# Two weight sums made by DMA chains, and the third product ahead of the fourth in a group's last pair

## The chip, the cores and the metric

The kernel runs on one core of one Trainium2 chip. The metric is the device time of one execution in microseconds (us). [...] In the rows of the profile, PE is the matrix engine and PEld its weight loads, DVE the vector engine, ACT the scalar engine, POOL the engine that here only issues the adding DMAs, and SP the one that issues the plain loads. Each engine works through its own list of instructions in order. An instruction that waits holds up everything behind it on its engine.

## The reference, cut to what matters

An encoder of two layers over 528 tokens (16 learned ones and 512 given ones) of width 1024. Each layer has two feed-forward blocks and a mixer between them; four feed-forward blocks in all.

```python
def swiglu(x, w_gate, w_up, w_down):
    return (jax.nn.silu(x @ w_gate) * (x @ w_up)) @ w_down

for l in range(DEPTH):                       # DEPTH = 2, D_FF = 2816
    h = h + 0.5 * swiglu(rmsnorm(h, norm_gains[l, 0]),
                         ffn_w_gate[l, 0], ffn_w_up[l, 0], ffn_w_down[l, 0])
    h = h + mixer(rmsnorm(h, norm_gains[l, 1]), ...)
    h = h + 0.5 * swiglu(rmsnorm(h, norm_gains[l, 2]),
                         ffn_w_gate[l, 1], ffn_w_up[l, 1], ffn_w_down[l, 1])
return rmsnorm(h, final_norm)[:, N_META:]
```

Everything is float32. The kernel splits each operand into a high part (a rounded copy, `hi`) and the rest (`lo`), and takes three products, hi·hi, hi·lo and lo·hi.

## The kernel before

**Seven products in place of eight.** The feed-forward blocks multiply 2 by 2 blocks by the Strassen-Winograd scheme. The 2816 hidden columns are cut into 11 *pairs* of 256 columns. For one pair there are seven block products with the names "1" to "7". Four blocks of weights w11, w12, w21 and w22, of 128 x 1024 elements (512 KB) each, feed them. Products "1", "2" and "4" take w11, w12 and w22 as they are. The others take sums: s1 = w21 + w22 for "5", s3 = w21 - w11 for "7", s2 = w22 + s3 for "6", s4 = s2 - w12 for "3". One product of a pair is 24 matmuls of 264 columns (256 in the last block): 16 with a hi of the weights and 8 with a lo. So is one S product; its part 1 is 18 of them and its part 2 is 6.

**Making weights.** `make` turns each 512 KB operand into hi (a cast on ACT, L287) and lo (a subtraction on DVE, L288) about three products ahead of its use. There are four buffers for each.

**Making sums.** The sums are made in one of two ways, in `begin_sums`, `sums` and `make`:

- *By a chain of DMAs*, for pairs 0 and 1 of every block (i < 2). ACT writes -w11 into a buffer (L203), POOL issues a DMA that adds w21 from memory to it (L208; this is s3), and then one that adds s3 to the loaded w22 (this is s2). In the same way s4 is made from -w12.
- *On DVE*, for pairs 2 to 10. SP loads w21, and DVE subtracts w11 from it (L253; s3) and adds it to w22 (L297; s2). s4 is a third subtraction on DVE (L256).

In both cases s1 is w21 loaded by SP, with w22 added by one POOL DMA.

**Order of the work.** `ffn_steps` writes out the order of the steps by hand. The pairs stand in three groups of 4, 4 and 3 (`GROUPS`). At the end of each of the first two groups (`FAST = 2`), the outputs of its four pairs are multiplied with the down weights, again by seven products ("S" steps, `fast_down`, L712), twice: `dq` 0 and 1. The first three of them, "1", "2" and "5", are cut in two: part 1 uses the outputs of the first three pairs, part 2 those of the last one. There are 4 blocks x 2 = 8 such group ends. "O" steps make the operands of the S products, `operand` on ACT (L673) and DVE (L674) and `difference` on DVE (L678).

**Inside a pair.** Accumulators X, Y and Z lie in PSUM. Products "1", "6", "7" and "4" add up in X one after the other; `snapshot` copies X to SBUF on ACT (L602) after "1", "6" and "7". "2" goes to Y. "5" and "3" add up in Z. DVE then forms the pair's output from the snapshots (L608 to L625), and `hidden` scales it (L642), takes silu on ACT (L444) and multiplies gate and up (L652). Half the output follows from "3" (m = 0, the raw quarters 0 and 1) and half from "4" (m = 1, the quarters 2 and 3). S product "1" needs quarter 0, "2" quarter 2, "5" the difference of quarters 1 and 0, and "6" quarter 3 minus that difference.

**The scheduler.** The instructions of an engine are put into their final order when the program is built, so a change of the steps can move other instructions of the same engine too.

Of the kernel before, what the change touches and what calls it, by code (L numbers as in the profile page):

```python
# [17 lines left out]
P = 128  # L18
# [22 lines left out]

GROUPS = (4, 4, 3)
FAST = 2
QUADS = 2
LATE = 5
HELD = 4
# [6 lines left out]
def ffn_steps(opening):  # L53

    steps, pair = [], 0
    for g, n in enumerate(GROUPS):

        ahead = g == 0  # L60
        begun = 0 < g <= FAST
        steps += [("P", p, c) for p in range(pair, pair + 1 + ahead) for c in "12"] * (not begun)
        early4 = (0, 1) if opening and ahead else ()
        steps += [("P", p, "4") for p in early4]
        steps += [("P", pair, c) for c in "65"] * (not begun)
        for i in range(n):
            p, more = pair + i, i + 1 < n
            early = [[("P", p + 1, "1")], [("P", p + 1, "2")]] if more else \
                [[("D", g, 0, 0, 2 * n - 2)], [("D", g, 1, 0, 2 * n - 2)]]
            if ahead and i == 0:  # L70
                early = [[], []]
            if not more and g < FAST:
                rest = [("S", g, 0, c, 2) for c in "125"]
                steps += [("O", g, 0), ("P", p, "7"), ("P", p, "4"), ("S", g, 0, "1", 1), ("P", p, "3")]
                steps += [("S", g, 0, c, 1) for c in "25"] + [("O", g, 1)] + rest
                turns = [("S", g, *t, 3) for t in zip(AB, "16273465734")]
                steps += turns[:6]
                for s, c in zip(turns[6:], "1265"):
                    steps += [s, ("P", p + 1, c)]
                steps.append(turns[-1])  # L80
                continue
            steps += early[0] + [("P", p, "7")] + early[1] + [("P", p, c) for c in "43" if c == "3" or p not in early4]
            if more:
                steps += [("P", p + 1, "6"), ("P", p + 1, "5")]
        if g >= FAST:
            steps += [("D", g, m, 0, 2 * n - 2) for m in range(2, HELD)]
            steps += [("D", g, m, 2 * n - 2, 2 * n) for m in range(HELD)]
            steps += [("D", g, m, 0, 2 * n) for m in range(HELD, KC)]
        pair += n
    return steps  # L90
# [80 lines left out]
class Weights:  # L171
# [34 lines left out]
    def add(self, t, src):  # L206

        self.nc.gpsimd.dma_start(t, src, accum_op=ALU.add)  # L208

    def begin_sums(self, f, i, w=None):  # L210

        got = self.summed
        s3 = None
        if i < 2:
            s3 = self.negative(f, i, "s3", w)
            self.add(s3, self.dram(f, i, "21"))
        elif i < NPAIR:
            s3 = self.block(f, i, "21", self.long, "wsa")
        s2 = self.block(f, i, "22", self.short, "wsb")
        if i < 2:  # L220
            self.add(s2, s3)
        got[f, i, "7"], got[f, i, "6"] = s3, s2
        if (f, i) not in OPENING:
            self.first_sum(f, i)
# [6 lines left out]
    def sums(self, f, i, product, w):  # L231


        got, V = self.summed, self.nc.vector
        if (f, i) in OPENING and product in "12":
            (self.begin_sums if product == "1" else self.first_sum)(f, i, *[w] * (product == "1"))
        if i < 2:
            if product == "2":
                s4 = self.negative(f, i, "s4", w)
                self.add(s4, got[f, i, "6"])  # L240
                got[f, i, "3"] = s4
        elif product == "1":
            if i < NPAIR:
                self.kept1 = w
            else:
                got[f, i, "7"] = self.negative(f, i, "s3", w)
                self.add(got[f, i, "7"], self.dram(f, i, "21"))
            if not i < NPAIR:
                self.add(got[f, i, "6"], got[f, i, "7"])
        elif product == "2":  # L250
            self.kept = w
            if i < NPAIR:
                V.tensor_tensor(got[f, i, "7"], got[f, i, "7"], self.kept1, ALU.subtract)  # L253
        elif product == "6":
            s4 = self.long.tile([P, SLAB], F32, tag="wsa", name=f"s4_{f[0]}{f[1]}_{i}")
            V.tensor_tensor(s4, w, self.kept, ALU.subtract)  # L256
            got[f, i, "3"] = s4
# [15 lines left out]
    def make(self, upto):  # L273
        nc = self.nc
        while self.made < min(upto, len(self.loads)):
            self.fetch(self.made + 1)
            s = self.made
            load = self.loads[s]
            w = self.raws.pop(s, None)
            if w is None:  # L280
                w = self.summed.pop(load)
            hi = self.hi_pool.tile([P, SLAB], F32R, tag="whi", name=f"whi{s}")
            lo = self.lo_pool.tile([P, SLAB], F32R, tag="wlo", name=f"wlo{s}")
            for a in np.split(np.arange(SLAB), 2 if s == 0 else 1):
                cs = slice(a[0], a[-1] + 1)
                with self.tc.issue_after(self.behind) if self.behind else nullcontext():
                    nc.scalar.copy(hi[:, cs], w[:, cs])  # L287
                nc.vector.tensor_tensor(lo[:, cs], w[:, cs], hi[:, cs].bitcast(F32), ALU.subtract)  # L288
            self.got[s] = (hi, lo)
            self.got.pop(s - 12, None)  # L290
            self.made += 1
            if not isinstance(load, int) and load[2] in "126":
                self.sums(*load, w)
            after = self.loads[s + 1] if s + 1 < len(self.loads) else 0
            if not isinstance(after, int) and after[2] == "6" and 2 <= after[1] < NPAIR:
                s2, s3 = [self.summed[after[:2] + (c,)] for c in "67"]
                nc.vector.tensor_tensor(s2, s2, s3, ALU.add)  # L297

# [30 lines left out]
def build(tc, ctx, xt, wts, win, par, w2, const, umask, out):  # L329
# [243 lines left out]
    def ffn(l, f, norm, done, following):  # L573
# [7 lines left out]
        def product_of_pair(p, product):  # L581
# [29 lines left out]
            elif apart:  # L611
                S.copy(part(st, 2), acc)
                st["apart"] = True
            elif product == "7":
                snapshot(3)
                if "apart" in st:
# [63 lines left out]
        def operands_of(g, ks, order):  # L680
            for c in order:
                if c == "5":
                    difference(g, 0, 1, 0, ks)
                operand(g, c, ks)
# [63 lines left out]
        for i, step in enumerate(steps):  # L748
# [14 lines left out]
            elif step[0] == "S":  # L763
                fast_down(*step[1:])
            elif step[0] == "O":
                g, last = step[1:]
                ks = slice(3, 4) if last else slice(0, 3)
                operands_of(g, ks, "215" if last else "125")
                difference(g, 0, 3, 0, ks)
                if last:  # L770
                    operand(g, "6")
            else:
                down(*step[1:])
# [597 lines left out]
```

## Time and profile before

| | us |
|---|---|
| median of 3 runs (2210.72 to 2214.04) | 2212.42 |
| the profiled execution | 2211.05 |
| its span, first to last instruction | 2209.2 |
| PE idle in the span (span less busy) | 46.8 |
| DVE busy | 1785.4 |
| ACT busy | 1214.1 |

The profiled execution took 2211.05 us by the same clock as the other runs; 1.9 us of it lie outside the span. Its mean granted TensorE clock was 0.997. In the rows of the timeline, the first number is the start in us from the beginning of the span and the second the length of the group; a bracket gives the time that the engine stood idle before the row and what released it. In the chain of work (the critical chain), the pieces follow one another without a gap: each begins when what it waited for has ended.

### The profile page before, as it was taken

What the parts mean: (1) busy time and instruction counts of PE and PEld (TensorE: products, weight loads), DVE (VectorE), ACT (ScalarE), POOL (GpSimd) and SP (SyncE); (2) the same over time, 40 slices, a digit from 0 to 9 for tenths busy, and PEclk for the clock granted to TensorE, in tenths of its full rate; (3) what the DMA queues carried; (4) which work ended last, traced back from release to release, by engine and by line L of the source; (5) the groups of instructions that cost most, each with busy time, mean ns of one, the idle gap of its engine ahead of it and who ended that gap; (6) DMA issues with size and microseconds to landing.
All of it is one profiled execution on the core that took longest, in us unless ns stands there. A gap on an engine that the chain in (4) does not pass through costs nothing.

```text
span 2209.2 us, 40079 instructions
## 1 busy us (share of the span) xinstructions
PE 2162.4 (98%) x16506; PEld 2070.2 (94%) x16506; DVE 1785.4 (81%) x2703; ACT 1214.1 (55%) x1779; POOL 101.8 (5%) x120
## 2 busy tenths in 40 slices
PE   7999999999999999999999999999999999999998
PEld 6999999989999999999999999999788888999997
DVE  7897978486886689889789979775879767997987
ACT  7544545344785555454575445453457836554543
POOL 1000000000000001000010000000000001000100
PEclk9999999999999999999999999999999999999999
DMA  9775753212113468666567757432121145776752
GB/s 268 189 204 160 191 152 106 82 49 68 49 39 122 114 167 205 190 182 187 162 163 186 207 164 191 143 110 77 49 84 51 42 133 152 198 202 181 189 165 67
DMA packets 87463, 311.41 MB, mean 141 GB/s; under 512 B 9712, under 2 KB 12144, under 8 KB 87280
## 3 DMA queue, kind: packets, MB, share of 16 engines
q1 hardware_dynamic: 68624, 245.53, 32.9%
q0 software_dynamic: 16704, 60.82, 15.8%
q8 instruction: 130, 2.13, 0.4%
q10 hardware_dynamic: 1952, 2.50, 0.4%
q14 instruction: 53, 0.43, 0.1%
HBM read 289.94 MB, written 2.10 MB: 132 GB/s over the span
## 4 chain that ended last, share of the span: by engine, by line
PE 81%; DVE 11%; ACT 4%; issue 2%; DMA 2%; SPq 0%; DVEq 0%; ACTq 0%
PE ss L598 37%; PE mm L465 13%; PE ss L712 11%; PE ss L465 10%; PE sm L465 2%; DVE wlo L288 2%; DMA w<-win 2%; PE sm L1074 1%; PE ss L1049 1%; DVE g L678 1%; ACT whi L287 1%; PE sm L1090 1%; DVE h L720 1%; PE ss L471 1%; PE sm L1091 1%
## 5 line engine op out<-in xcount | busy, mean ns | idle before, releaser
L598 PE MATMUL ss<-xc,whi 128*128 128x264 f32 (+1 forms) x4928 | 907.2, 285 | 15.5 <-ACT whi L287 7.4
L598 PEld LDWEIGHTS ss<-xc,whi 128*128 128x128 f32 x4928 | 767.2, 189 | 20.4 <-ACT c L602 8.4
L598 PE MATMUL ss<-xc,wlo 128*128 128x264 f32 (+1 forms) x2464 | 702.5, 285 | 8.8 <-DVE wlo L288 8.8
L598 PEld LDWEIGHTS ss<-xc,wlo 128*128 128x128 f32 x2464 | 466.5, 189 | 11.1 <-DVE wlo L288 10.9
L288 DVE TENSOR_TENSOR wlo<-w,whi 128x1024 fp32r<-128x1024 f32 (+1 forms) x337 | 408.1, 1217 | 63.4 <-ACT whi L287 63.2
L287 ACT CAST whi<-w 128x1024 fp32r<-128x1024 f32 (+1 forms) x337 | 350.0, 1050 | 163.3 <-PE ss L598 80.5
L465 PE MATMUL mm<-x,whi 128*128 128x264 f32 (+1 forms) x1712 | 384.6, 315 | 0.0
L465 PEld LDWEIGHTS mm<-x,whi 128*128 128x128 f32 x1712 | 278.3, 188 | 16.5 <-issue 1.0
L465 PE MATMUL mm<-x,wlo 128*128 128x264 f32 (+1 forms) x856 | 266.0, 315 | 0.0
L712 PE MATMUL ss<-g,whi 128*128 128x264 f32 (+1 forms) x1280 | 237.4, 284 | 0.0
L287 ACT CAST whi<-raw 128x1024 fp32r<-128x1024 f32 x126 | 132.3, 1050 | 163.4 <-PE mm L465 102.3
L602 ACT COPY c<-ss 128x528 f32<-128x528 f32 (+1 forms) x132 | 78.5, 594 | 258.6 <-PE ss L598 258.6
L288 DVE TENSOR_TENSOR wlo<-raw,whi 128x1024 fp32r<-128x1024 f32 x126 | 153.9, 1222 | 59.0 <-ACT whi L287 58.1
L712 PEld LDWEIGHTS ss<-g,whi 128*128 128x128 f32 x1280 | 198.4, 188 | 0.1
L712 PE MATMUL ss<-g,wlo 128*128 128x264 f32 (+1 forms) x640 | 181.3, 283 | 0.0
L465 PEld LDWEIGHTS mm<-x,wlo 128*128 128x128 f32 x856 | 159.6, 188 | 8.5 <-issue 0.7
L465 PE MATMUL ss<-g,whi 128*128 128x264 f32 (+2 forms) x900 | 166.3, 299 | 0.0
L465 PEld LDWEIGHTS ss<-g,whi 128*128 128x128 f32 x900 | 131.7, 188 | 5.3
L208 POOL DMA_DIRECT2D w<-win x60 | 52.7, 878 | 1574.7 <-DVE wlo L288 582.5
L712 PEld LDWEIGHTS ss<-g,wlo 128*128 128x128 f32 x640 | 120.5, 188 | 0.0
L444 ACT ACTIVATE c<-c 128x528 f32<-128x528 f32 (+1 forms) x88 | 56.6, 643 | 98.5 <-DVE c L642 98.4
L465 PE MATMUL ss<-g,wlo 128*128 128x264 f32 (+2 forms) x450 | 106.2, 300 | 0.0
(267 smaller groups left out, 3370.2 us busy)
## 6 DMA issues: line engine op xcount, KB each, us to landing
w<-win SPq DMA_DIRECT2D x335, 512.0 KB, 4.5
raw<-wts SPq DMA_DIRECT2D x126, 512.0 KB, 3.3
w<-win POOLq DMA_DIRECT2D x60, 512.0 KB, 7.4
s<-win POOLq DMA_DIRECT2D x24, 512.0 KB, 7.2
w<-s POOLq DMA_DIRECT2D x24, 512.0 KB, 5.6
s<-w POOLq DMA_DIRECT2D x8, 512.0 KB, 9.6
h<-xt SPq DMA_DIRECT2D x3, 528.0 KB, 6.8
out<-h ACTq DMA_DIRECT2D x4, 256.0 KB, 2.4
```

Source lines behind the costliest of these rows:

```text
L208: self.nc.gpsimd.dma_start(t, src, accum_op=ALU.add)
L287: nc.scalar.copy(hi[:, cs], w[:, cs])
L288: nc.vector.tensor_tensor(lo[:, cs], w[:, cs], hi[:, cs].bitcast(F32), ALU.subtract)
L444: prev_act[0] = S.activation(*args, **kw).ins
L465: TE.matmul(acc.half[i][:width], lhs, rhs[:, acc.spans[i]], start=first, stop=last)
L471: TE.matmul(a, weights, x[:, hs], start=True, stop=True)
L598: TE.matmul(acc[:, j], a[:, j, k], b[:, at], start=bool(begin and k == 0 and i == 0), stop=k == len(x) - 1 and i == 2, skip_group_check=no ...
L602: W.behind = S.copy(part(st, q), acc).ins
L678: V.tensor_tensor(r[into][:, ks], r[a][:, ks], r[b][:, ks], ALU.subtract)
L712: TE.matmul(acc[:, j], a[:, j, k], xs[b][:, k], start=bool(begin and k == 0 and i == 0), stop=k == 3 and i == 2, skip_group_check=not begin)
L720: V.tensor_tensor(to, to, acc, ALU.add)
L1049: TE.matmul(s[:n, i, :HF], lhs, kh[:, hs], start=True, stop=False)
```

## The change

It has two parts.

1. In the first block, (0, 0), pairs 2 and 3 get their s3 and s2 by the chain of DMAs (`chained`). For these pairs the loads of w21 for s3, the subtraction L253 and the addition L297 go; a negation on ACT and two adding DMAs each come in their place. s4 stays a subtraction on DVE.
2. At each of the eight group ends the last pair takes "3" before "4", and the S products stand in the order "1", "5", "2". For these last pairs the snapshot on ACT is taken of Z after "5", where one of X was taken after "7"; after "7" DVE adds X to it.

```diff
+LAST = [sum(GROUPS[: g + 1]) - 1 for g in range(FAST)]
...
-                rest = [("S", g, 0, c, 2) for c in "125"]
-                steps += [("O", g, 0), ("P", p, "7"), ("P", p, "4"), ("S", g, 0, "1", 1), ("P", p, "3")]
-                steps += [("S", g, 0, c, 1) for c in "25"] + [("O", g, 1)] + rest
+                rest = [("S", g, 0, c, 2) for c in "152"]
+                steps += [("O", g, 0), ("P", p, "7"), ("P", p, "3"), ("S", g, 0, "1", 1), ("P", p, "4")]
+                steps += [("S", g, 0, c, 1) for c in "52"] + [("O", g, 1)] + rest
...
+    def chained(self, f, i):
+        return i < 2 or f == (0, 0) and i < 4
...
-        if i < 2:
+        if self.chained(f, i):
             s3 = self.negative(f, i, "s3", w)
             self.add(s3, self.dram(f, i, "21"))
         elif i < NPAIR:
             s3 = self.block(f, i, "21", self.long, "wsa")
         s2 = self.block(f, i, "22", self.short, "wsb")
-        if i < 2:
+        if self.chained(f, i):
             self.add(s2, s3)
...
-        elif product == "1":
+        elif product == "1" and not self.chained(f, i):
             if i < NPAIR:
                 self.kept1 = w
...
-            if i < NPAIR:
+            if i < NPAIR and not self.chained(f, i):
                 V.tensor_tensor(got[f, i, "7"], got[f, i, "7"], self.kept1, ALU.subtract)
...
-            if not isinstance(after, int) and after[2] == "6" and 2 <= after[1] < NPAIR:
+            if not isinstance(after, int) and after[2] == "6" and after[1] < NPAIR and not self.chained(*after[:2]):
                 s2, s3 = [self.summed[after[:2] + (c,)] for c in "67"]
                 nc.vector.tensor_tensor(s2, s2, s3, ALU.add)
...
+            elif product == "5":
+                if p in LAST:
+                    snapshot(3)
+            elif product == "7" and p in LAST:
+                V.tensor_tensor(part(st, 3), part(st, 3), acc, ALU.add)
+                st["r"] = True
             elif product == "7":
                 snapshot(3)
...
-                operands_of(g, ks, "215" if last else "125")
+                operands_of(g, ks, "152")
```

**The opening of the first block.** In the names, w21_00_2 is block w21 of layer 0, block 0, pair 2; the last number is the tile's. DVE before, between the norm's factor (rs) and the second output of pair 0:

```order
L483 SCALAR_TENSOR_TENSOR rs44_521<-t46_528,rs44_521 128x528
L288 TENSOR_TENSOR wlo10_535<-w22_00_1_205,whi10_534 128x1024
L555 SCALAR_TENSOR_TENSOR rs47_532<-ss45_522,rs44_521 128x528
L253 TENSOR_TENSOR w21_00_2_376<-w21_00_2_376,w11_00_2_374 128x1024
L617 TENSOR_TENSOR c27_269<-c27_269 128x2x264
L288 TENSOR_TENSOR wlo11_577<-w21_00_1_276,whi11_576 128x1024
L618 TENSOR_TENSOR c27_269<-c27_269,ss43_492 128x2x264
L288 TENSOR_TENSOR wlo12_610<-w11_00_2_374,whi12_609 128x1024
L642 SCALAR_TENSOR_TENSOR c27_269<-c27_269,rs44_521 128x528
L288 TENSOR_TENSOR wlo13_649<-s3_00_1_202,whi13_648 128x1024
L297 TENSOR_TENSOR w22_00_2_378<-w22_00_2_378,w21_00_2_376 128x1024
```

The same place in the changed kernel:

```order
L486 SCALAR_TENSOR_TENSOR rs44_523<-t46_530,rs44_523 128x528
L558 SCALAR_TENSOR_TENSOR rs47_534<-ss45_524,rs44_523 128x528
L291 TENSOR_TENSOR wlo10_537<-w22_00_1_205,whi10_536 128x1024
L768 SCALAR_TENSOR_TENSOR h_82<-h_82,rs47_534 128x528 x2
L626 TENSOR_TENSOR c27_269<-c27_269 128x2x264
L291 TENSOR_TENSOR wlo11_579<-w21_00_1_276,whi11_578 128x1024
L627 TENSOR_TENSOR c27_269<-c27_269,ss43_494 128x2x264
L291 TENSOR_TENSOR wlo12_612<-w11_00_2_374,whi12_611 128x1024
L651 SCALAR_TENSOR_TENSOR c27_269<-c27_269,rs44_523 128x528
L291 TENSOR_TENSOR wlo13_653<-s3_00_1_202,whi13_652 128x1024
```

The subtraction that forms s3 of pair 2 (L253) and the addition to s2 (L297) are gone; two scalings of h stand where L253 stood. On POOL, the list of adding DMAs was this:

```order
L208 DMA w21_00_1_276<-win 128x1024
L208 DMA s4_00_1_279<-w22_00_1_205 128x1024
L208 DMA w21_00_2_380<-win 128x1024
L208 DMA w21_00_3_619<-win 128x1024
L208 DMA s3_00_11_1134<-win 128x1024
```

and is now this:

```order
L209 DMA w21_00_1_276<-win 128x1024
L209 DMA s4_00_1_279<-w22_00_1_205 128x1024
L209 DMA s3_00_2_376<-win 128x1024
L209 DMA w22_00_2_379<-s3_00_2_376 128x1024
L209 DMA w21_00_2_382<-win 128x1024
L209 DMA s3_00_3_617<-win 128x1024
L209 DMA w22_00_3_620<-s3_00_3_617 128x1024
L209 DMA w21_00_3_623<-win 128x1024
```

Each of the pairs 2 and 3 has its two new DMAs ahead of the one that it had; the s1 of pair 2 is now behind the chain of its s2. ACT gets the two negations: that of pair 2 directly ahead of the cast for product "6" of pair 1, that of pair 3 ahead of the cast for "2" of pair 2.

**A group's end** (the first one; c59 and c60 belong to the last pair's two outputs, g48 to g51 are the quarters 0 to 3, c66/c68 and c73 are lo of the operands "5" and "6"). DVE before, from the last product of the pair, "3", on:

```order
L625 TENSOR_TENSOR c59_906<-c59_906,ss62_1086 128x2x264
L642 SCALAR_TENSOR_TENSOR c59_906<-c59_906,rs44_521 128x528
L288 TENSOR_TENSOR wlo31_1261<-w11_00_12_1053,whi31_1260 128x1024
L652 TENSOR_TENSOR g48_570<-c59_906 128x264
L652 TENSOR_TENSOR g49_571<-c59_906 128x264
L674 TENSOR_TENSOR g64_1117<-g48_570,g63_1116 128x264
L678 TENSOR_TENSOR g48_570<-g49_571,g48_570 128x264
L678 TENSOR_TENSOR g49_571<-g49_571,g51_573 128x1056
L674 TENSOR_TENSOR c68_1126<-g48_570,c67_1125 128x264
```

and in the changed kernel, where "4" is the last product:

```order
L259 TENSOR_TENSOR s4_00_11_1291<-w22_00_11_914,w12_00_11_1018 128x1024
L651 SCALAR_TENSOR_TENSOR c60_906<-ss58_876,rs44_523 128x264
L291 TENSOR_TENSOR wlo31_1261<-w11_00_12_1053,whi31_1260 128x1024
L661 TENSOR_TENSOR g50_574<-c60_906,ss58_876 128x264
L661 TENSOR_TENSOR g51_575<-c60_906 128x264
L683 TENSOR_TENSOR g64_1118<-g48_572,g63_1117 128x264
L683 TENSOR_TENSOR g68_1127<-g50_574,g67_1126 128x264
L687 TENSOR_TENSOR g48_572<-g49_573,g48_572 128x264
L687 TENSOR_TENSOR g49_573<-g49_573,g51_575 128x1056
L683 TENSOR_TENSOR c66_1123<-g48_572,c65_1122 128x264
```

The last piece now scales half a tile (264) where it added and scaled whole ones (528); the s4 of the down weights, which stood ahead of the old last piece, stands directly before the new one, and the lo of operand "2" has moved into the list. Behind these rows both kernels have the same six rows: an addition to h, the lo of the weights of S product "6" (wlo32), the `difference` for operand "6", two more additions to h, and the lo of operand "6" (c73). On ACT the same stretch reads, before:

```order
L673 CAST g63_1116<-g48_570 128x264
L673 CAST c67_1125<-g48_570 128x264
L287 CAST whi32_1287<-w22_00_11_915 128x1024
L287 CAST whi33_1354<-w12_00_12_1138 128x1024
L287 CAST whi34_1388<-s3_00_11_1134 128x1024
L673 CAST c72_1328<-g48_570 128x1056
```

and in the changed kernel

```order
L682 CAST g67_1126<-g50_574 128x264
L682 CAST c65_1122<-g48_572 128x264
L290 CAST whi32_1287<-w22_00_11_914 128x1024
L290 CAST whi33_1354<-w12_00_12_1139 128x1024
L290 CAST whi34_1388<-s3_00_11_1135 128x1024
L682 CAST c72_1328<-g48_572 128x1056
```

Here the three casts of weights stay ahead of the cast of operand "6" (c72); only the operand whose quarter comes last, "2" for "1", has changed.

More of the change, by code (lines that the diff above doesn't have):

```diff
@@ L247, in sums @@
                 self.add(got[f, i, "7"], self.dram(f, i, "21"))
-            if not i < NPAIR:
                 self.add(got[f, i, "6"], got[f, i, "7"])
```

## The prediction

> **What bounds the kernel now.** I read the page first, for the engines' shares, then the waits of PE, then the timeline at each place that the change touches, and last the chain of waits through one group's end.
>
> ```profile
> span 2209.2 us, 40079 instructions
> PE 2162.4 (98%) x16506; PEld 2070.2 (94%) x16506; DVE 1785.4 (81%) x2703; ACT 1214.1 (55%) x1779; POOL 101.8 (5%) x120
> ...
> PE ss L598 <- DVE wlo L288: 8.8, 8, 3.1
> PE ss L598 <- ACT c L602: 6.1, 11, 0.7
> PE ss L712 <- DVE c L674: 3.4, 8, 0.6
> ```
>
> PE is busy for 98% of the span, and no matmul is removed. All that can be won is PE's idle time, 46.8 us, and time in which PE runs slowly. The three waits below the engines' row (total, times, longest) are the ones that the change can reach. The two longest of the first kind lie in the first block:
>
> ```profile
> 53.58 0.59 PE L598 MATMUL ss<-xc,wlo 128*128 128x264 f32 x1 [3.15 <-DVE wlo L288]
> 69.34 0.39 PE L598 MATMUL ss<-xc,wlo 128*128 128x264 f32 x1 [2.36 <-DVE wlo L288]
> ...
> 50.54 1.23 DVE L253 TENSOR_TENSOR w<-w,w 128x1024 f32<-128x1024 f32 x1 [3.42 <-DMA w<-win]
> 52.30 1.22 DVE L288 TENSOR_TENSOR wlo<-w,whi 128x1024 fp32r<-128x1024 f32 x1
> 66.24 1.23 DVE L253 TENSOR_TENSOR w<-w,w 128x1024 f32<-128x1024 f32 x1 [4.92 <-DMA w<-win]
> 68.07 1.22 DVE L288 TENSOR_TENSOR wlo<-w,whi 128x1024 fp32r<-128x1024 f32 x1
> ...
> 48.56 2.00 ACT L287 CAST whi<-w 128x1024 fp32r<-128x1024 f32 x2 [0.66 <-DMA w<-win]
> ```
>
> PE waits for a lo of weights, but the lo isn't slow: DVE stands still at L253, the first subtraction of a pair's s3, until the load of w21 has landed, and the lo that PE needs is queued behind. These stalls cost more than their length:
>
> ```profile
> 50.00:53.41 3.41, 0.43 (x4) 0.22 (x2) 2.87 (x3) 3.28 (x4) 0.00 (x0) 1.00 0.10 19
> 53.41:56.82 3.41, 3.24 (x14) 3.25 (x15) 3.41 (x5) 0.65 (x1) 0.07 (x1) 0.50 0.86 291
> 70.48:73.89 3.41, 3.41 (x17) 3.29 (x16) 3.41 (x5) 0.43 (x1) 0.00 (x0) 0.50 0.15 36
> 73.89:77.30 3.41, 3.41 (x28) 3.32 (x28) 3.41 (x7) 1.26 (x2) 0.00 (x0) 1.00 0.80 253
> ...
> 53.58 13.18 PE ss L598 x94
> 69.34 36.87 PE ss L598 x286
> 154.70 2.93 PE ss L598 x24
> ```
>
> In the table of stretches, the number before the last two is the granted clock. After each stall it is 0.50 for 3.41 us, with 14 and 17 matmuls done where an undisturbed stretch has 28. At full speed 24 matmuls take 2.93 us, 0.122 each: the 94 behind the first stall would take 11.5 and took 13.18 (1.7 lost), the 286 behind the second 34.9 and took 36.87 (2.0 lost).
>
> The other two waits are one place, eight times. In the chain of waits it reads, for the first group:
>
> ```profile
> 106.29 0.61 ACT c L602
> 106.94 3.19 PE ss L598 x24
> 110.14 1.95 PE ss L712 x16
> 112.09 2.94 PE ss L598 x24
> 115.05 0.71 DVE c L625
> 116.42 1.22 DVE wlo L288
> 119.39 1.26 DVE g L678
> 121.00 0.61 DVE h L720
> 124.32 1.24 DVE c L674
> 125.60 1.47 PE ss L712 x10
> ```
>
> From the end of product "7" (106.29) to S product "6" (125.60) the path is: the snapshot of "7" on ACT (PE idle meanwhile), "4", part 1 of S "1", "3", and then 10.5 us on DVE and ACT until the lo of operand "6" is there (115.05 to 125.56), while PE runs out of work.
>
> **Part 1, the chains.** Removed: four DVE subtractions and additions of 1.23 us and, with them, DVE's two waits for w21. Added: two negations on ACT, and two adding DMAs for each pair on POOL. The gain first. PE loses 3.15 + 2.36 idle and 1.7 + 2.0 slow, 9.2 us. Of the first stall some is left: the hi of the same weights is cast in the group that starts at 48.56, its own share 1.0; a lo of 1.22 behind it ends at 50.8, and PE stopped at 53.58 - 3.15 = 50.4. That leaves 0.4. At the second place DVE then has 18 instructions (by the order, from the first lo to this one) for about 11.2 us, so the lo is there at 62.1, and PE, with 94 matmuls of 0.122 after 50.8, needs it at 62.4: nothing left in the middle, 0.2 taken. With 0.3 for two slow restarts, 0.9 stays.
>
> What the added work may cost depends on when it lands:
>
> ```profile
> 43.23 0.65 ACT L444 ACTIVATE t<-rs 128x528 f32<-128x528 f32 x1
> 37.04 1.05 ACT L203 ACTIVATE s<-w 128x1024 f32<-128x1024 f32 x1
> 43.35 0.89 POOL L208 DMA_DIRECT2D s<-w  x1 [3.14 <-ACT rs L444]
> 47.30 0.60 ACT L602 COPY c<-ss 128x528 f32<-128x528 f32 x1 [2.47 <-PE ss L598]
> s<-win POOLq DMA_DIRECT2D x24, 512.0 KB, 7.2
> w<-s POOLq DMA_DIRECT2D x24, 512.0 KB, 5.6
> s<-w POOLq DMA_DIRECT2D x1, 512.0 KB, 9.4
> w<-win POOLq DMA_DIRECT2D x2, 512.0 KB, 9.2
> ```
>
> The first negation (1.05) stands behind the row at 43.23 and ends at 44.9. It pushes one cast of hi and one lo to 47.1; PE takes them at 47.3, when "7" of pair 0 ends. POOL is free then (43.35 + 0.89). Two adds in a row follow: at the medians of the page, 7.2 + 5.6, with 0.4 each for POOL to start, s2 lands at 58.5; at the 9.4 and 9.2 that the two kinds took in just this stretch (40 to 70 us, where constants and weights crowd in), at 64.3. PE asks for product "6" of pair 2 one product (2.93) after 62.4, at 65.4, and a hi takes 1.05: needed by 64.4. I take a wait of 0.7, since the upper end is the nearer row and just meets the need; the bounds are 0 and, with both adds a third longer, 6 and a slow stretch. Pair 3's chain follows 15 us later on POOL for a product ("6") that comes 23 us later: free. What hides the rest of the added work is the 3 products by which weights are made ahead. Sum of part 1: 9.2 - 0.9 - 0.7 = **7.6 us won**, bounds 1 and 9.
>
> [...]
>
> **Part 2, a group's end.** Removed from the path: the snapshot (106.29 to 106.94, 0.65) and the slow start of "4" after it (3.19 against 2.93, 0.26), 0.91 in all. Product "3" goes to Z, whose snapshot was taken a product earlier, and starts at once. "4" goes to X behind DVE's addition of X, which has "3" and part 1 of S "1" (2.93 + 1.95) as its cover. Then the path is the same length on PE, and DVE's and ACT's stretch behind the last product decides. Its DVE rows: one scaling of half a tile where an addition (0.71) and a whole scaling stood, about 1.0 less; an extra lo of 264 columns, 0.35 more; and the s4 subtraction of 1.2, which is moved to directly ahead, with about 0.7 of it behind the end of "4". That is as long as before, 10.5. ACT then counts: three casts of hi, 1.05 each, wait for PE to free the weights of "1", "5" and "2", and the cast of operand "6" stands behind them. The part 2 of "1" ends 0.91 earlier than before, but that of "5" now waits for its lo, which is not earlier by as much; I place that cast, and so S "6", 0.4 later than the full gain. So 0.5 of 0.91, and 0.15 from the restarts: 0.65 for each group's end, with bounds 0 (all goes into the wait for operand "6") and 1.35:
>
> ```profile
> 125.60 0.39 PE L712 MATMUL ss<-c,whi 128*128 128x264 f32 x1 [0.40 <-DVE c L674]
> 125.60 11.92 PE ss L712 x96
> 2075.56 0.39 PE L712 MATMUL ss<-c,whi 128*128 128x256 f32 x1 [0.55 <-DVE c L674]
> ```
>
> 0.40 and a restart of 0.2 (96 matmuls of 0.122 are 11.7) is all that waits there besides. The stall is the same at every end, up to 0.55 at the last. **8 x 0.65 = 5.2 us won.** The DMAs that swap places in SP's and POOL's lists are loads and adds for S products that come 8 us and more later; nothing.
>
> **Sum.** The profiled execution, 2211.05, becomes 2211.05 - 7.6 - 5.2 = 2198.25. The median of the runs shown lies 1.37 above that execution, so 2199.6. About 0.2% (4.4 us) is what a measurement of this kernel can tell from no change.
>
> **Rivals.**
>
> *The chain lands late.* PE waits 2.5 us for s2 of pair 2 and a slow stretch follows (1.7). For it: the adds take 9.4 where DMAs crowd. Against: two loads are gone from the same stretch. 2199.6 + 4.2 = 2203.8. Chance 0.15.
>
> *The wait at a group's end only moves* to the lo of "5" or "6", or product "4" still waits: part 2 is worth nothing, as its chain of 10.5 us behind the last product stays. 2199.6 + 5.2 = 2204.8. Chance 0.14.
>
> *The slow stretches stay*, because their cause isn't the stall: 2199.6 + 3.7 = 2203.3. Against it are the windows above. Chance 0.04. [...]
>
> *Both at once*: pair 2 late by 2.5 with a slow stretch of 1.7, pair 3 by 1.5, and nothing won at the ends: 2199.6 + 4.2 + 1.5 + 5.2 = 2210.5, no change. Chance 0.07.
>
> *Slower:* ACT's list at a group's end. Three casts wait for slots, and operand "6" behind them; if the last quarter of "2", now last, ends late, because its own lo stands behind the s4 subtraction and the lo of the next weights, each us is paid eight times. It begins to cost from 0.65 later than I place it, and outweighs part 1 by 0.2% from 0.65 + (7.6 + 4.4) / 8 = 2.2 us. With 3 us: 8 x (3 - 0.65) - 7.6 = 11 more, 2223. Against: only 1.26 and 1.22 stand ahead, not 3. Chance 0.08.
>
> **How the numbers follow.** The forecast has 0.52 (2192 to 2203). Faster by more than 0.2% are the forecast and the first three rivals, 0.85; no change 0.07; slower 0.08. The range 2191 to 2208 leaves out the last two rivals and a little on the fast side (part 1 at 9, part 2 at 1.35 each gives 2192.6).
>
> **What would show it.** Right: no wait of over 1 us on DVE's lo between 45 and 75 us, both stretches at clock 0.50 gone, L253's two DMA waits gone; at the ends no wait on ACT's snapshot before the product behind "7", eight fewer in that row, while the wait of S products for operands stays or grows. PE's busy time falls by some 3.7 us of slow matmuls, its idle time by the rest. Wrong: a wait for a cast that itself waits for an adding DMA near 65 us; a wait at the S products of over 1.3 us at each end.

## The result, and the profile after

| | before | after |
|---|---|---|
| median, us | 2212.57 (6 runs, 2208.98 to 2215.25) | 2197.61 (6 runs, 2196.04 to 2198.96) |
| ratio after/before | | 0.9932, 95% interval 0.9920 to 0.9944 |
| span of the profiled execution | 2209.2 | 2194.3 |
| PE busy / idle in the span | 2162.4 / 46.8 | 2157.0 / 37.3 |

The change won 15.0 us where 12.8 were predicted; the time is 2.0 us under the forecast. The page's head and the engines' row after:

```profile
span 2194.3 us, 40087 instructions
...
PE 2157.0 (98%) x16506; PEld 2066.7 (94%) x16506; DVE 1777.9 (81%) x2699; ACT 1215.5 (55%) x1781; POOL 105.3 (5%) x124
```

The same matmuls, 5.4 us less of busy time and 9.5 us less of idle time. The waits of PE (engine, line, the releaser; total, times, longest, in us):

```profile
PE ss L721 <- DVE c L683: 3.4, 8, 0.5
PE ss L601 <- DVE wlo L291: 3.3, 6, 0.8
...
PE ss L601 <- ACT c L605: 2.1, 3, 0.7
```

L601, L291, L605, L721 and L683 are the lines that were L598, L288, L602, L712 and L674. The wait for DVE's lo fell from 8.8 to 3.3 us, with none over 0.8; the wait for ACT's snapshot from 11 times to 3. The eight waits of the S products are as they were. The stretches that ran at half clock, in the table of stretches (PE, PEld, DVE, ACT, POOL busy with counts, then the granted clock, the DMA share and GB/s):

```profile
50.00:53.41 3.41, 3.34 (x28) 3.13 (x27) 3.41 (x5) 3.30 (x4) 0.09 (x1) 1.00 0.92 250
53.41:56.82 3.41, 3.41 (x31) 3.41 (x30) 3.41 (x7) 0.62 (x2) 1.64 (x2) 1.00 0.99 298
...
70.48:73.89 3.41, 3.41 (x31) 3.41 (x30) 2.44 (x3) 2.50 (x4) 0.86 (x1) 1.00 1.02 249
```

Both are gone: 31 matmuls at clock 1.00 where 14 and 17 stood at 0.50.

**The new chain is on the path, but barely.** The chain of waits of the changed kernel through the first block (start, length, what):

```profile
44.21 0.81 POOL s L209
45.02 7.91 DMA s<-win
52.93 0.39 issue
53.32 10.18 DMA w<-s
...
63.59 0.10 DVE s L259
63.69 1.05 issue
64.73 0.71 DVE c L627
65.44 0.04 issue
65.48 23.44 PE ss L601 x190
```

The two adds of pair 2 end one behind the other at 63.50. DVE's subtraction for s4 (L259) waits for that landing, the addition that reads the accumulator Z (L627) stands behind it, and product "3" of pair 1 needs Z free. PE loses 0.5 us there by the starts of its matmuls, idle and in slowed ones.

**A group's end after.** The chain through the first one, where S product "6" started at 125.60 before:

```profile
109.68 0.36 DVE g L687
...
110.06 1.26 DVE g L687
111.32 0.34 DVE c L683
111.66 0.61 DVE h L729
112.28 1.14 DVE wlo L291
113.41 0.34 DVE g L687
113.76 1.23 DVE h L729 x2
114.98 1.24 DVE c L683
116.22 0.04 issue
116.27 5.85 PE ss L721 x46
```

"6" starts at 116.27, 9.33 earlier. At the last of the eight ends it starts 14.97 earlier (2075.56 before, 2060.59 now), so each end in between won (14.97 - 9.33) / 7 = 0.81. With one such end in it, the first 9.33 leave 8.5 for the chains.

### The profile page after: what moved, and what is told of

Its sections match the earlier page's. It is cut to its first block, busy times and chain, and to the rows that moved or that the text cites. A ratio compares the mean times of both kernels' runs of the same rounds, so it can differ in the third digit from the quotient of the medians.

```text
span 2194.3 us, 40087 instructions
## 1 busy us (share of the span) xinstructions
PE 2157.0 (98%) x16506; PEld 2066.7 (94%) x16506; DVE 1777.9 (81%) x2699; ACT 1215.5 (55%) x1781; POOL 105.3 (5%) x124
## 4 chain that ended last, share of the span: by engine, by line
PE 76%; DVE 16%; ACT 4%; issue 2%; DMA 2%; SPq 0%; POOL 0%; DVEq 0%; ACTq 0%
PE ss L601 33%; PE mm L468 13%; PE ss L721 11%; PE ss L468 10%; DVE wlo L291 4%; PE sm L468 2%; DVE g L687 1%; PE sm L1083 1%; DVE c L683 1%; DVE g L683 1%; PE ss L1058 1%; DVE c L651 1%; DMA w<-win 1%; DVE g L661 1%; PE ss L474 1%
## 5 line engine op out<-in xcount | busy, mean ns | idle before, releaser
L601 PE MATMUL ss<-xc,whi 128*128 128x264 f32 (+1 forms) x4928 | 903.4, 285 | 11.6 <-ACT whi L290 7.4
L601 PEld LDWEIGHTS ss<-xc,whi 128*128 128x128 f32 x4928 | 764.8, 189 | 14.9 <-ACT whi L290 7.8
L601 PE MATMUL ss<-xc,wlo 128*128 128x264 f32 (+1 forms) x2464 | 700.7, 285 | 3.4 <-DVE wlo L291 3.3
L601 PEld LDWEIGHTS ss<-xc,wlo 128*128 128x128 f32 x2464 | 465.1, 189 | 5.2 <-DVE wlo L291 5.2
L291 DVE TENSOR_TENSOR wlo<-w,whi 128x1024 fp32r<-128x1024 f32 (+1 forms) x335 | 405.5, 1217 | 64.1 <-ACT whi L290 63.9
L721 PE MATMUL ss<-g,whi 128*128 128x264 f32 (+1 forms) x1280 | 237.0, 284 | 0.0
L605 ACT COPY c<-ss 128x528 f32<-128x528 f32 (+1 forms) x132 | 78.5, 595 | 245.7 <-PE ss L601 245.3
L291 DVE TENSOR_TENSOR wlo<-raw,whi 128x1024 fp32r<-128x1024 f32 x126 | 153.9, 1222 | 59.3 <-ACT whi L290 58.4
L721 PEld LDWEIGHTS ss<-g,whi 128*128 128x128 f32 x1280 | 198.4, 188 | 0.1
L721 PE MATMUL ss<-g,wlo 128*128 128x264 f32 (+1 forms) x640 | 181.3, 283 | 0.0
L721 PEld LDWEIGHTS ss<-g,wlo 128*128 128x128 f32 x640 | 120.5, 188 | 0.0
L291 DVE TENSOR_TENSOR wlo<-s,whi 128x1024 fp32r<-128x1024 f32 x86 | 104.9, 1220 | 1.7 <-ACT whi L290 1.5
```

The costliest lines, as they stand in the source:

```text
L601: TE.matmul(acc[:, j], a[:, j, k], b[:, at], start=bool(begin and k == 0 and i == 0), stop=k == len(x) - 1 and i == 2, skip_group_check=no ...
L605: W.behind = S.copy(part(st, q), acc).ins
L721: TE.matmul(acc[:, j], a[:, j, k], xs[b][:, k], start=bool(begin and k == 0 and i == 0), stop=k == 3 and i == 2, skip_group_check=not begin)
```

## The experiments

| run | median, us | before beside it | ratio, 95% interval |
|---|---|---|---|
| e1, chains only | 2203.14 | 2211.23 | 0.9964, 0.9950 to 0.9977 |
| e2, ends only | 2204.70 | 2211.23 | 0.9973, 0.9964 to 0.9983 |
| e3, one chain | 2210.71 | 2211.23 | 0.9997, 0.9988 to 1.0006 |
| e4, old snapshot | 2203.04 | 2211.23 | 0.9965, 0.9951 to 0.9979 |
| e5, old order | 2208.91 | 2210.04 | 0.9993, 0.9984 to 1.0002 |
| e6, "7" later | 2201.44 | 2210.04 | 0.9967, 0.9955 to 0.9980 |
| e7, late constants | 2197.22 | 2210.04 | 0.9946, 0.9933 to 0.9958 |
| e8, long stalls | 2253.02 (one run) | 2210.04 | |
| e9, "7" on POOL | 2208.29 | 2211.11 | 0.9988, 0.9978 to 0.9997 |
| e10, "6" on POOL | 2197.15 | 2211.11 | 0.9936, 0.9924 to 0.9949 |
| e11, both on POOL | 2224.89 | 2211.11 | 1.0051, 1.0037 to 1.0064 |
| e12, short stalls | 2201.05 (one run) | 2211.11 | |

The kernel before ran again in three batches, with e1 to e4, e5 to e8 and e9 to e12. Its median was 2210.04 to 2211.23 there and 2212.57 beside the change, so a difference of 1 or 2 us between runs of different batches means little.

### The two parts apart (e1, e2)

e1 has only the chains, with the old order and the old snapshot at the ends.

> Part 1 alone: pairs 2 and 3 of the first block by chains, the group ends as before. My theory, from the two profiles (PE reached the first group's S product 6 at 125.60 us before and at 116.27 after, of which one group end is about 0.8): 8.5 us of the 15 come from here, so about 2204.1 against 2212.6. Both half-clock stretches are gone, the waits at the group ends are those of the kernel before: 0.5 on the snapshot and 0.4 on operand 6, eight times. Rival, that the parts need one another (a group's end gains only because DVE is freed by the chains): then this run is worth clearly more or less than 8.5 and the two parts alone do not add up to 15.

e2 has only the ends:

```diff
-        return i < 2 or f == (0, 0) and i < 4
+        return i < 2
```

> Part 2 alone: the new order and the new snapshots at the group ends, the sums of pairs 2 and 3 on DVE as before. My theory: 0.8 for each of eight ends, 6.4 us, about 2206.2 against 2212.6; the two stalls of 3.15 and 2.36 us on DVE's lo and both half-clock stretches are there as before. Rival: as for the chains alone, a sum of the two that is not 15; or, if the stall in the opening were tied to the order of the ends, other lengths of the two stalls.

Beside the same runs of before, e1 won 8.1 us and e2 6.5; the sum, 14.6, is the change's 15.0 within the intervals. The waits of PE in e1:

```profile
PE ss L601 <- ACT c L605: 6.1, 11, 0.7
...
PE ss L601 <- DVE wlo L291: 3.3, 6, 0.8
```

and in e2:

```profile
PE ss L601 <- DVE wlo L291: 8.6, 9, 2.6
...
PE ss L601 <- ACT c L605: 2.1, 3, 0.7
```

Each run has one of the two rows as before and the other as after. e2 also kept both stretches at half clock, and e1 has none: they belong to the stalls. Two stretches of e2 in the table, each inside a slow one:

```profile
53.80:57.00 3.20, 3.20 (x16) 3.20 (x16) 3.20 (x4) 0.65 (x1) 0.88 (x1) 0.50 0.86 220
70.80:73.90 3.10, 2.92 (x14) 2.61 (x12) 3.10 (x5) 0.81 (x1) 0.00 (x0) 0.50 0.20 46
```

### One chain of the two (e3)

```diff
-        return i < 2 or f == (0, 0) and i < 4
+        return i < 2 or f == (0, 0) and i < 3
```

with the ends as before.

> The chains for pair 2 alone, the sums of pair 3 on DVE, the group ends as before. My theory: the first stall (3.15 and 1.7 of slow clock) goes, but DVE's next wait, for the w21 of pair 3, does not end earlier by as much as PE now comes earlier, since that load is tied to DMA and to free buffers: the second stall grows from 2.36 to 4 us or more, and no more than 3 us are won, 2209.5 or more. Rival, that the two stalls are independent prices: 4.5 us are won, 2208.1, and the second stall stays at 2.4.

With only pair 2 by DMAs nothing is won. The timeline of e3 at the second place, for DVE and then for PE:

```profile
66.60 1.23 DVE L256 TENSOR_TENSOR w<-w,w 128x1024 f32<-128x1024 f32 x1 [7.62 <-DMA w<-win]
...
69.70 0.59 PE L601 MATMUL ss<-xc,wlo 128*128 128x264 f32 x1 [5.98 <-DVE wlo L291]
```

The load of w21 of pair 3 lands about when it did (DVE goes on at 66.60, at 66.24 before), while all that stands ahead of it is done earlier. DVE waits 7.62 where it waited 4.92, and PE 5.98 where it waited 2.36. Taking away the first stall alone only brought PE early to the second one, so the 9.2 us of the prediction come only if both go.

### The two halves of the ends (e4, e5)

The change with the old snapshot (e4):

```diff
-            elif product == "5":
-                if p in LAST:
-                    snapshot(3)
-            elif product == "7" and p in LAST:
-                V.tensor_tensor(part(st, 3), part(st, 3), acc, ALU.add)
-                st["r"] = True
```

> The change with the old snapshot: product 3 ahead of 4, but X is copied on ACT after 7 and DVE adds Z to the copy. My theory: the order alone wins nothing, since 3 adds to Z and must now wait for the copy (0.6) and for DVE's addition that reads Z (0.7): PE waits about 1.3 us plus a slow restart of 0.26 ahead of 3, against none in the change, 8 x 1.5 = 12 us lost: about 2209.5 against the change's 2197.6, worse at the ends than the kernel before. Rival, that the order is what wins (later product with a free accumulator) and the snapshot matters little: within 2 us of 2197.6.

The change with the old order (e5):

```diff
-                steps += [("O", g, 0), ("P", p, "7"), ("P", p, "3"), ("S", g, 0, "1", 1), ("P", p, "4")]
-                steps += [("S", g, 0, c, 1) for c in "52"] + [("O", g, 1)] + rest
+                steps += [("O", g, 0), ("P", p, "7"), ("P", p, "4"), ("S", g, 0, "1", 1), ("P", p, "3")]
+                steps += [("S", g, 0, c, 1) for c in "25"] + [("O", g, 1)] + rest
...
-                operands_of(g, ks, "152")
+                operands_of(g, ks, "215" if last else "125")
```

> The change with both chains and with its two snapshots from the sum in PSUM, but with the old order in a group's last pair (product "4" ahead of "3", remainders 2, 1, 5 and then 1, 2, 5). Theory 1 (the snapshot and the order work only together: with the old order product "4" needs VectorE's addition of X directly behind "7", some 0.75 to 1 us late, where ScalarE's copy was 0.65 late): within 1 us of the chains alone (2203.1), so 2202 to 2205, with eight waits of TensorE at L601 on VectorE's addition or snapshot. Theory 2 (the second read of PSUM in place of ScalarE's copy is what wins, the order is not needed): within 1.5 us of the change, 2196 to 2199.

All four combinations, with the chains in each: both old 2203.1 (e1), new order alone 2203.0, new snapshot alone 2208.9, both new 2197.6. Neither half wins by itself, and the new snapshot alone loses 5.8 us (7.0 when e1 and e5 are each taken against the runs of before beside them), more than theory 1 allowed. The code shows why neither wins. In e4 product "3" goes to Z, which DVE reads only behind ACT's copy of X; in e5 product "4" goes to X, which DVE still has to read. In both, the scheduler moved matmuls of S "1" ahead of that product to fill the gap: 8 of 18 in e4, 15 of 18 in e5 (counted from the trace at the first end). In e4 PE then waits for their lo, and is 5.4 us over the change, less than was expected:

```profile
PE ss L715 <- DVE wlo L291: 12.5, 8, 1.6
```

In e5 S "1" no longer stands between "4" and "3" (3 matmuls are left of it), so DVE and ACT begin the second output with less cover, and S "6" waits longer than the 0.38 of the change:

```profile
118.08 0.39 PE L721 MATMUL ss<-c,whi 128*128 128x264 f32 x1 [0.60 <-DVE c L683]
```

Where e5 loses its time can be read from the starts of the matmuls. From 94 us to the start of S "6" at the first end, PE stands still or runs slowly for 2.54 us in e5, 1.62 in e1 and 0.81 in the change. Eight times the 0.92 between e5 and e1 is 7.4, so the loss lies at the ends, and 1.5 of the 2.54 stand ahead of S products from 116 us on. That it is the moved matmuls that bring these waits was not tested.

### What is left at the ends (e6, e9, e10, e11)

e6 puts the subtraction for operand "7" behind the lo of operand "6":

```diff
-                difference(g, 1, 1, 3)
+                with after(six[0]):
+                    difference(g, 1, 1, 3)
```

> The change, with VectorE's subtraction for operand "7" of the last group's next pair issued only behind the remainder of operand "6" in each group's last pair, so that the remainders of S "5" and "6" come one subtraction earlier. Theory 1 (what is left at each group's end is that VectorE reaches the remainders of "5" and "6" late, because the subtraction for "7" stands ahead of them): the eight waits at L721 on VectorE (3.4 us in all) and the small ones ahead of them go, some 0.5 to 0.7 us per end: 2192 to 2194. Theory 2 (VectorE is simply behind by one subtraction at the end of each group, whatever its order): the wait moves on to S "7" with the same length, 2196.5 to 2199.

3.8 us slower than the change. The timeline of PE at the first end of e6 (two rows):

```profile
121.34 0.39 PE L728 MATMUL ss<-g,whi 128*128 128x264 f32 x1 [0.26 <-DVE g L689]
...
128.35 0.39 PE L728 MATMUL ss<-g,whi 128*128 128x264 f32 x1 [0.40 <-DVE g L689]
```

The wait at S "6" is gone, and in its place PE waits at S "7" and again at "4". Theory 2 holds there, in a worse form than expected: one wait became two. All waits of S products for DVE together are 4.4 us, where the change has 3.4. The larger part of the loss is elsewhere: at the last two ends PE waits 0.94 and 2.04 us for a cast of weights on ACT, and why that comes late there was not looked into.

e9, e10 and e11 take the work off DVE in place of moving it:

```diff
-            V.tensor_tensor(r[into][:, ks], r[a][:, ks], r[b][:, ks], ALU.subtract)
+            E = G if into == 1 else V
+            E.tensor_tensor(r[into][:, ks], r[a][:, ks], r[b][:, ks], ALU.subtract)
```

(e10: `(into, a, ks.stop) == (0, 3, 3)` as the condition; e11: either of the two.)

> The change, with one operation per group's last pair taken from VectorE and given to GpSimd: the subtraction of 128 x 1056 for operand "7", which stands on VectorE (1.25 us) just ahead of the remainders of S "5" and "6". Theory 1 (at the group ends VectorE simply has too much to do, and what is left there goes with its work): the waits at S "5" and S "6" (0.16 and 0.55 us per end in the change) go and do not come back later, 0.6 to 0.7 us per end: 2192 to 2193. Theory 2 (the wait only moves on to the next remainder, as it did when the same subtraction was put behind): 2196.5 to 2202. Theory 3 (GpSimd's subtraction is slow enough to be late for operand "7", or VectorE is slowed beside it): a new wait at S "7", 2197 to 2210.

> The change, with the first part (128 x 792, 0.98 us on VectorE) of the subtraction for operand "6" in a group's last pair given to GpSimd. It stands on VectorE directly ahead of the addition of X, which product "1" of S and the snapshots wait for, and its result is needed some 14 us later, so GpSimd has time for it. Theory 1 (VectorE is behind throughout the group's end): 0.6 to 0.7 us per end are won, 2192 to 2193, with no wait left at S "6". Theory 2 (the remainders at S "5" and "6" hang on what comes after: the products "4" and "3" and the operands' last parts set their start, so work taken away 10 us earlier does nothing): 2196.5 to 2198.5.

> Both subtractions of the two runs before on GpSimd: some 2.1 us of VectorE's work less per end. Theory 1 (VectorE's work sets the ends): no wait of TensorE over 0.2 us left there, 2191 to 2193, no better than with one alone, since one is more than the 0.7 us that are left. Theory 2 (each helps another part of the end): better than either alone by 1 to 3 us. Theory 3 (GpSimd's work beside VectorE's costs it as much as it takes off): 2197 or more.

e9 lost 10.7 us against the change. Its timeline at the first end, POOL and then DVE:

```profile
111.62 2.83 POOL L688 TENSOR_TENSOR g<-g,g 128x1056 f32<-128x1056 f32 x1
...
112.39 3.16 DVE L291 TENSOR_TENSOR wlo<-w,whi 128x1024 fp32r<-128x1024 f32 x1
115.47 1.25 DVE L683 TENSOR_TENSOR c<-g,c 128x1056 fp32r<-128x1056 f32 x1
```

POOL works from 111.62 to 114.45. DVE's lo starts in that time and takes 3.16 us instead of the 1.22 that this operation took in the kernel before: it ends at 115.55, 1.1 us behind POOL, as if it had stood still until then. Taking an operation of 1.25 off DVE cost it 1.94. So theory 3 of e9 holds, by DVE being held up and not by POOL being late. In e11 the victim is a lo of an operand:

```profile
111.73 2.83 POOL L688 TENSOR_TENSOR g<-g,g 128x1056 f32<-128x1056 f32 x1
...
112.13 3.56 DVE L683 TENSOR_TENSOR c<-g,c 128x1056 fp32r<-128x1056 f32 x1
...
117.58 0.48 PE L722 MATMUL ss<-c,whi 128*128 128x264 f32 x2 [2.53 <-DVE h L730]
```

With 3.56 in place of 1.25 all that stands behind it on DVE is late, PE waits 2.53 us ahead of S "6", and a stretch at half clock follows at every end. That makes e11 slower than the kernel before; theory 3 holds there too. POOL ends at 114.56 and DVE's lo at 115.69, 1.1 behind it as in e9. What in the hardware holds DVE up, no run shows.

In e10 POOL works 10 us earlier:

```profile
97.44 2.80 POOL L688 TENSOR_TENSOR g<-g,g 128x792 f32<-128x792 f32 x1 [3.30 <-DVE c L683]
...
98.40 0.70 DVE L621 TENSOR_TENSOR c<-c,ss 128x528 f32<-128x528 f32 x1
99.01 3.45 DVE L291 TENSOR_TENSOR wlo<-w,whi 128x1024 fp32r<-128x1024 f32 x2
```

The addition that reads PSUM isn't disturbed (0.70, as in the change, where it stands at 99.33), but two lo of 1.22 take 3.45: some 1.0 is given back of the 0.98 that was taken off. The wait at S "6" went, and one came 12 us later:

```profile
128.03 0.39 PE L722 MATMUL ss<-c,wlo 128*128 128x264 f32 x1 [0.42 <-DVE wlo L291]
```

2197.15 beside the change's 2197.61 is no difference: theory 2's time, but not its reason, since the remainder of "6" did come early enough. In e6 and e10 alike the wait for DVE moved on. That DVE's total work at the ends sets it fits these four runs, but a kernel with less work on DVE and none on POOL was not tried.

### The constants beside the chain (e7)

The loads of three tables of constants are issued two pairs later:

```diff
-            if pending:
+            if pending and p == 3:
```

> The change, with the loads of the three tables of constants issued two pairs later. Theory 1 (the second chain's adding transfer takes 10.2 us and lands at 63.5 us because the constants' loads run beside it from 52.7 us on): it lands at 60 to 62 us, VectorE's subtraction of s4 waits for it no longer, the step of 0.39 us of TensorE at 65.5 us goes: 0.3 to 0.5 us won, 2197.1 to 2197.3, and in the trace the adding transfer takes 9.0 to 9.6 us. Theory 2 (the adds are slow by themselves or by the weights' own loads): landing still 63 to 64 us, time within 0.2 us.

The add took 8.0 us instead of 10.18 and landed at 60.9 instead of 63.5 (the issues and landings in the trace), so some 2.2 us of it came from the three loads beside it. Yet PE's step at the place stayed. The chain of waits of e7:

```profile
62.43 0.37 DVE s L259
62.80 0.77 issue
63.57 0.70 DVE c L626
64.27 1.15 DVE wlo L291
65.42 0.04 issue
65.46 4.54 PE ss L601 x35
```

No DMA is in it any more: DVE's own list takes as long. The time, 2197.22, is the change's. The wait has two causes of equal length, and taking one away wins nothing.

### Which stalls halve the clock (e8, e12)

Multiplications with no use are put into DVE's list ahead of product "6" of some pairs (eight in e8, four in e12); nothing of the computation changes. In the built programs they stand earlier than that: in e8 they are gathered in three places, from 786, 1154 and 1900 us on, and the six of e12's first block run at 44 to 52 us. So e8 has three places with stalls in place of eight.

> The change with VectorE kept busy by 8, 10, 11, 12, 13, 14, 16 and 18 multiplications of 128 x 528 with no use (0.62 us each) just ahead of the product "6" of eight pairs far apart, so that TensorE stalls for different lengths at places where nothing else is late. Theory 1 (TensorE loses half its rate for one window of about 3.4 us when most of one such window was idle: 92% and 67% were in the kernel before): stalls under 2 us are followed by none, stalls over 4 us always by one, those between 2 and 4 us by their place in the window; each such stretch costs about 1.7 us on top of the stall. Theory 2 (any stall of over 1 us brings it): stalls from 1 us up are all followed by one. Theory 3 (only an idle stretch of a whole window does): stalls under 3.4 us never bring one.

> The change with VectorE kept busy by 3, 4, 5 and 6 multiplications of 128 x 528 with no use (0.62 us each) ahead of product "6" of one pair in each of the four blocks. The longer chains before (8 and more) gave stalls of TensorE of 4.9 to 12.5 us, each followed by some 20 matmuls at half rate; the kernel before had half rate behind 3.15 and 2.36 us, and 1.99 us had none. Expected stalls of about 1.8, 2.4, 3.0 and 3.7 us. Theory 1 (most of one window of 3.4 us must be idle): half rate behind those of 3.0 us and more, 2.4 us by its place, none behind 1.8 us. Theory 2 (a whole window must be idle): none behind those under 3.4 us.

In e8 the long ones gave stalls of 4.9 to 12.5 us, none shorter; in e12 two of the four showed, as 2.25 and 1.34 us, and two were hidden by other work. So neither run alone covers the range, but with the other runs there is a list. The gap is the start of a matmul less the end of the step before it (0.122 behind that start); at half rate the steps are 0.22 long:

| gap of PE, us | where | matmuls at half rate behind it |
|---|---|---|
| 1.3 to 1.5 | e9, four ends; e12, one place | none |
| 1.70 to 1.79 | e4, eight ends | none |
| 1.57 to 2.08 | all runs but e3, the opening, at 39 to 41 us | none |
| 2.07 | e3, the opening | 16 |
| 2.19 | e6, the last end | none |
| 2.22 | e9, the second end | 15 |
| 2.25 | e12 | none |
| 2.52, 3.30 | before | 14, 13 |
| 2.65, 2.74 | e2 | 15, 12 |
| 2.69 to 2.95 | e11, six ends | 13 to 15 |
| 2.99; 3.43, 3.55 | e9; e11, two ends | 22; 24, 12 |
| 6.15 | e3 | 25 |
| 4.9 to 12.45 | e8, three places | 19 or 20 |

The stretches of e11 at the first end, by the grid on which its clock changes:

```profile
115.37:118.78 3.41, 1.20 (x10) 1.23 (x11) 3.41 (x6) 3.00 (x4) 0.00 (x0) 1.00 1.00 209
118.78:122.20 3.42, 3.42 (x18) 3.42 (x17) 3.42 (x4) 1.13 (x2) 0.00 (x0) 0.50 0.38 137
```

A window with PE busy for 1.20 of 3.41 us is followed by one at 0.50. Theory 1 holds for the stalls, and theories 2 and 3 fall. A gap of 2.07 or 2.22 brought half rate, and gaps of 2.08, 2.19 and 2.25 did not, so the length alone doesn't decide. In the record of the granted clock of the kernel before, both stretches at 0.50 are 3.413 us long, and the 13.653 between them are four times that. In e12's record the two changes, at 20.41 and 2191.29, lie 636 such windows apart, which gives the edges around its gap of 2.25 (47.28 to 49.53):

```profile
44.31:47.72 3.41, 3.13 (x26) 2.92 (x24) 3.41 (x7) 1.90 (x3) 1.78 (x2) 1.00 0.82 156
47.72:51.13 3.41, 1.60 (x13) 1.60 (x14) 3.41 (x5) 2.80 (x4) 0.00 (x0) 1.00 1.07 185
```

The gap is shared out to two windows, and the worse one still has PE busy for 1.60 us. The gap of 2.22 in e9 lies in one window and leaves it 1.35.

**Half rate without a stall.** The profiles of e3 to e6 and e9 to e11 have one more stretch at 0.50, in the first mixer (at 559 to 574 us), behind a window in which PE was busy for all of 3.41 us. There, 16 of 29 matmuls have only 2 columns. So the sum of columns of the matmuls that begin in a window is the better measure here. An undisturbed window has 28 matmuls of 264, 7392 columns. The fourteen traces have 8817 windows at full rate between 20 and 2180 us (2230 in e8). All 18 with at most 2168 columns were followed by half rate, and none with more than 3168 was. Of the windows between these two numbers 8 were and 37 were not; what decides there stays open. The window of 1.60 us above has 3432 columns, the one in e9 2376.

## Why the prediction was right, and where it was off

**Part 1, the mechanism.** Right: stalls, half-clock stretches and DVE's waits for w21 in the first block all went. The sum was 7.6; e1 measured 8.1, the trace 8.5. The gain of 9.2 was about right; the two deductions, 0.9 and 0.7, were too large. What stays, by the starts of the matmuls, is 0.3 at 50.35 and 0.5 at 65.48, 0.8 in all. One argument was missing: 9.2 was added up from two stalls as if each could be had by itself, and e3 shows that the first alone is worth nothing within what the runs can tell.

**Part 1, the late chain.** s2 was to land between 58.5 and 64.3, and landed at 63.50. The wait was put at ACT's cast for product "6" of pair 2, 0.7 us. It came at another place: through DVE's s4 subtraction, which reads s2 too, and the addition of Z behind it, for product "3" of pair 1. I had named what the cast waits for, but not what else reads s2 and what is queued behind that. That the wait came out at 0.5, near the 0.7, is luck. The rival with 2.5 us of lateness didn't come.

**Part 2, 0.65 per end.** The mechanism was right, and the term mis-sized: 0.81 measured. The removed 0.91 was read somewhat too high: by the starts of the matmuls, e1 has a gap of 0.66 ahead of "4" and 0.10 in its slow first matmul, 0.76, which the change has not. The step that failed is "ACT then counts", which set 0.4 against it: in the chain after there is no piece of ACT ahead of S "6", only DVE, and S "6" starts earlier by the whole of what was removed. The rival that ACT's list is late falls with it, and so does the one that the wait at the ends only moves (e2: 6.5 us won). The prediction didn't see that the two edits of part 2 need each other (e4, e5); it costed them as one, which is why that did no harm.

**The half-clock stretches.** Right: they came from the stalls and went with them (none in e1, both in e2), and the rival in which they stay falls. A window need not be idle throughout: at e11's first end one with PE busy for 1.20 of 3.41 us was followed by one at 0.50, and in seven runs one with PE busy for all of 3.41 was.

**PE's busy time** was to fall by 3.7 and fell by 5.4. The parts apart have 2158.7 (e1, 3.7 less than before) and 2160.5 (e2, 1.9 less), so the chains gave the 3.7 and the ends the rest, about 0.24 at each. That these are the matmuls slowed behind the waits that went (0.39 in place of 0.28 in such rows) is argued, not shown.

## What to carry to other kernels

- When a stall is to be removed, ask whether the next one is the same lateness seen again: where both hang on transfers whose landing the edit doesn't move, a stall removed at the first place comes back at the second (in e3, PE's 2.36 us there became 5.98).
- Before moving a product behind another, look at which accumulator it writes and which engine still has to read that. Order and snapshot are one decision; half of it won nothing here, or lost 6 to 7 us.
- Where several causes of a wait are equally late, taking away one shows nothing in the time (e7, 2197.22 beside 2197.61). Look for the next piece in the chain of waits before paying for the edit.

## What was not expected of the hardware

- Beside a subtraction of 2.83 us on POOL with all operands in SBUF, two of DVE's operations with two SBUF inputs took 3.16 us (e9) and 3.56 us (e11) instead of 1.22 and 1.25. DVE's addition that reads PSUM took its usual 0.70 beside one of 2.80 (98.40 in e10).
- The same adding DMA of 512 KB from POOL's queue, the last of pair 2's chain, took 10.18 us in the change, with three loads of constants beside it, and 8.0 in e7, where they are issued two pairs later.
- In the fourteen traces, all 18 windows of 3.41 us at full rate with at most 2168 columns, where an undisturbed one has 7392, were followed by one at half rate, and none above 3168 was. A stretch at half rate cost some 1.5 us on top, an estimate from the 14 and 17 matmuls of 0.122 us that such stretches of the kernel before have in place of 28. All stalls of 2.52 us and more in the list brought it; of those of 2.07 to 2.25, two did and three did not; and in seven runs it followed a window with 16 matmuls of 2 columns and no stall.
